# Recurrence of a four-mixer network: quarter-array products over four quarters, sums ahead of transposing, and a planner that keeps the time of each quarter

## The chip, the cores and the metric

The kernel runs on one core of a Trainium2 chip. The metric is the device time of one execution in microseconds (us); the times given are medians over executions.

The engines are called as the profile calls them: PE is TensorE (matrix products), PEld its loading of weights, DVE is VectorE, ACT is ScalarE, POOL is GpSimd, SP is SyncE, which issues most of the transfers. PSUM is the memory that PE writes into; it is used in banks of 128 x 512 float32, named `ps`. PE's array has 128 rows and 128 columns. A product with 64 rows and 64 columns of weights uses a quarter of the array, one with 128 rows and 64 columns half of it.

## The reference

One sequence of 512 tokens and width 1024 goes through four layers, each a mixer and a feed-forward part with the residual around both. The mixers are of four kinds: RWKV-7, attention in a window of 128 with sinks, a gated unit over chunks, and gated linear attention. The change is in the first of them, the RWKV-7 mixer, and in three helpers. Its core:

```python
def rmsnorm(x, g):
    y = x * lax.rsqrt(jnp.mean(jnp.square(x), -1, keepdims=True) + NORM_EPS)
    return y * g

def rwkv7_mix(x, ...):                    # 16 heads of 64
    ...                                   # r, w, k, v, a, g from products of x with weights
    def step(state, inp):                 # one token; state is 64 x 64 for each head
        r_t, d_t, k_t, v_t, kk_t, a_t = inp
        sa = jnp.einsum('bhvk,bhk->bhv', state, kk_t)
        state = (state * d_t[:, :, None, :]
                 - sa[..., None] * (kk_t * a_t)[:, :, None, :]
                 + v_t[..., None] * k_t[:, :, None, :])
        return state, jnp.einsum('bhvk,bhk->bhv', state, r_t)
    _, y = lax.scan(step, zeros, xs)
    ...                                   # mean and variance of y in each head
    y = ((y - mean) * lax.rsqrt(var + RW_GN_EPS)).reshape(B, S, D) * gn_g + gn_b
    bonus = (jnp.sum(r * k * r_k, -1, keepdims=True) * v).reshape(B, S, D)
    return ((y + bonus) * g) @ w_o
```

## The kernel before

**The program and its order.** The kernel is written as operations on engines that a class `Program` records (all of them through one helper, so that every operation has that helper's line in the profile: L365 before, L370 after). `Program.run` then sets the order by a simulated list schedule: each operation has a cost in ns and a turn, which is its number plus an offset from the table `TURNS` (ranges of numbers, each with an offset); of the operations that could start, the one with the earliest start, and among those the lowest turn, is taken next. The buffers come from pools with a fixed count, and the plan waits for a free one. Where PE would idle in the plan, `keep_warm` and `ahead_of_cold` put in products of the identity with itself (`ident`), whose results nobody uses; they are recorded at a line of their own (L647 before, L665 after) and are called fills here. Every engine then runs its list in this order on the chip; only semaphores make it wait there.

**Large products.** A product with float32 weights splits weights and tokens in two parts of fewer bits (`whi`, `wlo` from the loaded `wraw`), and multiplies them one by one. Nearly all time outside the recurrence goes to these.

**The start.** The mean of squares of each token is needed first. `token_squares` loads `x` by tokens in eight tiles (`slot<-x`), and squares and sums each on ACT or DVE; the vectors (`t<-vecs`) and the transposed `x` (`h<-x_t`) are loaded behind them. `rsqrt` computes 1/sqrt on DVE by three steps of Newton from an integer guess, `rstd` carries the factor of each token to a row over all partitions by products with the identity (`ident,rcol`), `h<-h,vec,ps` scales the tokens, and the first weight product (`slot,whi`) follows.

**The RWKV mixer.** After the products for k and r (`rf`, `kf`, 16 tiles named `rk`) the 16 heads go in four groups of four. For group `n`, `prepare(n)` makes decays and factors; `ahead(n)` makes the products of tokens with each other in chunks of 64 (`rwkv_products`, into `pr`/`pa`), the inverse of a triangular 64 x 64 block for each chunk and head (`rwkv_inverse`, by blocks of 16: two levels, each with 32 + 32 products of 64 x 64), and the direct part. `rwkv_chain(n)` then goes over the 512 tokens in eight steps (`b` of 0 to 3, `c` of 0 and 1), with the group's state `st` of 128 x 256:

- `ab`: products of `pa` with `v`, for two `b` at once; `xb`: products of the inverse (`iv`) with these;
- `x` gets the product of `qk` with the state; `vu` is copied from it by ACT;
- `pb`: the state by way of a product with the identity (`st,ident`, two of 128 x 128), to which four products `vu,et` of 64 x 64 are added; DVE multiplies by the decay `pend` into the next `st` (one operation of 128 x 256, or two of 64 x 128 for the first step of a group);
- four products `vu,pa` of 64 x 64 add the output `y` of the step.

`rwkv_out` normalises `y` in each head, transposes `y` and the bonus term (`yt`, `bt`, four transposes each for two `b`), and adds, scales and gates them on the transposed side. The chain of group `n` is recorded behind `prepare` and `ahead` of the next group, and the table mixes them. Then `rwkv_out_proj` multiplies the six first tiles with `rw_w_o` in the buffers of the recurrence (`et`), `stream` opens the buffers for large weights (`wraw` in the pool `wr`, eight of them, with `whi` and `wlo`), and `out_proj` does the last two tiles with these.

**In the first groups two of the four quarters work at a time:** the products of `ab` alternate between `(rows low, columns high)` and the opposite, those of `xb` between the other two; `vu,pa` of one step stay in one column half:

```python
halves = (lo, hi), (hi, lo)
...
mm(ab[ru, k * W:][:, hc(i, h)], pc(i, h, c, 1 - c, b + k)[rv], sb['v'][b + k][rv, hc(i, h)], ...)
mm(xb[:, c * W:(c + 1) * W][ru, hc(i, h)], inv(i, h)[ru], w1[ru, hc(i, h)], ...)
mm(x[rv, hc(i, h)], pc(i, h, c, c), vu[:, hc(i, h)], start=False, stop=True)
```

Of the kernel before, what the change touches and what calls it, by code (L numbers as in the profile page):

```python
# [9 lines left out]
F32 = mybir.dt.float32  # L10
# [7 lines left out]
P = 128  # L18
S = 512
# [301 lines left out]
class Program:  # L321

    WINDOW, SLACK, SEM, LOAD = 700, 200.0, 100.0, 95.0
    FREE, GAP, TAIL, TURN = 4, 450.0, 150.0, 92.0
    TICK, BUSY, DENSE, RICH = 10240 / 3, 3000.0, 3000.0, 4200.0

    def __init__(self, tc):  # L330
# [1924 lines left out]
```

## Time and profile before

| | |
|---|---|
| median of 3 executions | 2393.93 us (2393.26 to 2398.78) |
| the profiled execution | 2394.06 us, of which the span of the trace 2392.4 us |
| busy share of the span | PE 98%, PEld 82%, DVE 80%, ACT 60%, POOL 14% |
| granted TensorE clock | 9 tenths or more in all 40 slices of the page |
| transfers | 407.64 MB, mean 170 GB/s |

The profile is read in four stretches of the first layer's time, since only there something changes: the start until the first weight product (0 to 19.2 us), the dense products for r, k, v with the first group's preparation mixed into their end (to 222), the recurrence (222 to 380), the output projection (380 to 425). The other 1967 us hold the first feed-forward part and the other three layers. In a row of the timeline stand start, duration, engine, line, operation, `out<-in`, form, count, and in brackets how long the engine had been idle before it and on whom it waited.

### The profile page before, as it was taken

To read this page: it belongs to the slowest core of one execution; us is meant where nothing else is said; L and a number is where in the kernel's file an instruction comes from. 1 tells how busy PE (TensorE), PEld (TensorE's weight loads), DVE (VectorE), ACT (ScalarE), POOL (GpSimd) and SP (SyncE) were. 2 spreads that over 40 slices of the span, in tenths; PEclk is the share of its full clock that TensorE was granted. 3 is DMA by queue.
4 is the path that set the end of the run, shared out by engine and by line. 5 is a ranking of instruction groups with operands and counts; after the bars stand their busy time and mean duration, and the time that the engine had idled before them with its cause. 6 is when DMAs were issued, how large, how long until landed. Compare 5 with 4: busy or idle time off the path is not lost.

```text
span 2392.4 us, 36503 instructions
## 1 busy us (share of the span) xinstructions
PE 2354.2 (98%) x13756; PEld 1949.9 (82%) x13756; DVE 1913.3 (80%) x2974; ACT 1433.2 (60%) x2351; POOL 323.9 (14%) x388
## 2 busy tenths in 40 slices
PE   9999999999999999999999999999999999999998
PEld 7677789988888769888877888988888888888886
DVE  7687775886889789868688887877868978886868
ACT  4467784765556587655474444765556856765545
POOL 0000000211121011212121100212111111211211
PEclk9999999999999999999999999999999999999999
DMA  5220011889988268898888745888998877889885
GB/s 176 75 69 8 7 35 58 217 214 232 226 204 198 54 158 200 206 233 209 222 208 200 209 96 153 188 223 215 213 227 195 187 182 154 189 197 229 211 218 124
DMA packets 127681, 407.64 MB, mean 170 GB/s; under 512 B 14576, under 2 KB 19696, under 8 KB 127504
## 3 DMA queue, kind: packets, MB, share of 16 engines
q0 software_dynamic: 52992, 180.38, 42.2%
q1 hardware_dynamic: 74512, 224.93, 27.4%
q8 instruction: 108, 1.77, 0.3%
q14 instruction: 69, 0.57, 0.1%
HBM read 400.79 MB, written 2.10 MB: 168 GB/s over the span
## 4 chain that ended last, share of the span: by engine, by line
PE 87%; DVE 6%; ACT 4%; DMA 1%; issue 1%; SPq 0%; ACTq 0%; DVEq 0%
PE ps L365 87%; ACT et L365 2%; DVE slot L365 2%; ACT slot L365 1%; DVE wlo L365 1%; DVE et L365 1%; DMA wraw<-sg_w_u 1%; DVE h L365 0%; ACT whi L365 0%; DVE mx L365 0%; ACT vu L365 0%; DMA wraw<-ffn_w_b 0%; DMA slot<-x 0%; DVE ps L365 0%; DMA et<-rw_w_o 0%
## 5 line engine op out<-in xcount | busy, mean ns | idle before, releaser
L365 PE MATMUL ps<-whi,slot 128*128 128x512 f32 (+1 forms) x4944 | 1501.3, 384 | 0.5 <-DVE slot L365 0.3
L365 PEld LDWEIGHTS ps<-whi,slot 128*128 128x128 f32 x4944 | 918.7, 188 | 174.7 <-issue 7.8
L365 ACT CAST whi<-wraw 128x1024 fp32r<-128x1024 f32 (+2 forms) x683 | 677.8, 999 | 620.0 <-PE ps L365 518.9
L365 DVE TENSOR_TENSOR wlo<-wraw,whi 128x1024 fp32r<-128x1024 f32 (+2 forms) x683 | 782.8, 1157 | 233.1 <-ACT whi L365 223.8
L365 PE MATMUL ps<-wlo,slot 128*128 128x512 f32 (+1 forms) x2472 | 929.1, 383 | 1.4 <-DVE wlo L365 1.4
L365 PEld LDWEIGHTS ps<-wlo,slot 128*128 128x128 f32 x2472 | 463.8, 188 | 83.4 <-DVE wlo L365 5.0
L365 PE MATMUL ps<-slot,whi 128*128 128x512 f32 (+1 forms) x912 | 258.0, 369 | 5.2 <-ACT whi L365 2.3
L365 PEld LDWEIGHTS ps<-slot,whi 128*128 128x128 f32 x912 | 163.3, 190 | 39.7 <-ACT whi L365 4.8
L365 DVE TENSOR_TENSOR slot<-ps,slot 128x512 f32<-128x512 f32 (+1 forms) x238 | 150.3, 648 | 45.0 <-PE ps L365 41.2
L365 DVE TENSOR_TENSOR h<-h,ps 128x512 f32<-128x512 f32 x256 | 168.6, 684 | 18.6 <-PE ps L365 17.2
L365 POOL DMA_DIRECT2D wraw<-ffn_w_a x128 | 113.6, 893 | 480.6 <-DVE wlo L365 366.3
L365 DVE TENSOR_TENSOR slot<-left,slot 128x512 fp32r<-128x512 f32 (+1 forms) x252 | 159.9, 658 | 11.8 <-ACT slot L365 8.7
L365 PE MATMUL ps<-slot,wlo 128*128 128x512 f32 (+1 forms) x456 | 164.5, 367 | 0.8 <-DVE wlo L365 0.8
L365 ACT CAST slot<-left 128x512 fp32r<-128x512 f32 (+1 forms) x252 | 143.3, 599 | 33.7 <-DVE left L365 28.2
L365 ACT COPY slot<-ps 128x512 f32<-128x512 f32 (+2 forms) x157 | 82.8, 544 | 49.9 <-PE ps L365 39.0
L365 POOL DMA_DIRECT2D wraw<-ffn_w_b x64 | 55.9, 884 | 419.2 <-PE ps L365 224.1
L365 DVE TENSOR_TENSOR slot<-slot 128x512 f32<-128x512 f32 (+4 forms) x157 | 93.2, 617 | 11.0 <-DMA slot<-slot 6.5
L365 PEld LDWEIGHTS ps<-slot,wlo 128*128 128x128 f32 x456 | 85.7, 189 | 18.9 <-DVE wlo L365 3.0
L365 POOL DMA_DIRECT2D wraw<-ffn_o_a x64 | 55.3, 864 | 285.7 <-DVE wlo L365 176.9
L365 PE MATMUL ps<-ident,slot 128*128 128x128 f32 x524 | 87.0, 274 | 2.1 <-ACT slot L365 1.7
L365 DVE SCALAR_TENSOR_TENSOR slot<-slot,ncol 128x512 f32<-128x512 f32 (+1 forms) x96 | 66.8, 704 | 12.7 <-ACT slot L365 11.8
L365 PEld LDWEIGHTS ps<-ident,slot 128*128 128x128 f32 x524 | 62.9, 140 | 15.7 <-ACT slot L365 3.9
(282 smaller groups left out, 2085.3 us busy)
## 6 DMA issues: line engine op xcount, KB each, us to landing
wraw<-ffn_w_a SPq DMA_DIRECT2D x128, 512.0 KB, 5.9
wraw<-ffn_w_a POOLq DMA_DIRECT2D x128, 512.0 KB, 7.9
wraw<-ffn_o_a SPq DMA_DIRECT2D x64, 512.0 KB, 5.0
wraw<-ffn_o_a POOLq DMA_DIRECT2D x64, 512.0 KB, 7.0
wraw<-ffn_w_b SPq DMA_DIRECT2D x64, 384.0 KB, 5.4
wraw<-ffn_w_b POOLq DMA_DIRECT2D x64, 384.0 KB, 6.5
wraw<-ffn_o_b SPq DMA_DIRECT2D x16, 512.0 KB, 4.6
wraw<-ffn_o_b POOLq DMA_DIRECT2D x16, 512.0 KB, 6.8
```

The costliest lines, as they stand in the source:

```text
L365: op = self.add(eng.name, lambda: getattr(eng.target, what)(*map(real, args), **{k: real(a) for k, a in kw.items()}), *self.price(eng.name ...
```

## The change

1. **Planner.** `Program.run` keeps a time for each quarter of the array (`self.array`). A product of a quarter or half occupies its own quarters for its cost and lets PE go on after 13.5 ns (`STEP`); a change of form waits for all quarters and costs 92 ns from the full form or 140 ns into another (`shape`). Before, such a product cost half as much if the one ahead of it lay in the other half. The fills follow these times.
2. **TURNS** is a new table for the whole program, since the numbers of all operations move.
3. **Start.** `token_squares(xs)` takes the tiles of the transposed `x` (`h<-x_t`, now loaded first); the eight loads of `x` go. ACT squares the eight tiles, and PE sums over partitions by 32 products with one column of ones (`onec,slot`), into one PSUM column for each 128 tokens.
4. **`rsqrt`**, used in all layers: one step of higher order and one of Newton, eight DVE operations in place of ten.
5. **Pools.** `pa` and `mt` get pools of their own, `et` has 22 buffers instead of 30; `wr`, the raw weights' eight buffers, is opened before the last group's chain instead of in `stream`.
6. **`rwkv_inverse`.** The 64 x 64 products of both levels go round the four quarters (`turns`); the identity is added by a product `eye` at both levels (sixteen in place of eight), so that ACT copies the result of the first where DVE added.
7. **`rwkv_chain`.** The products of `ab` are recorded between those of `xb` (`other`). `st,ident` becomes four products of 128 rows and 64 columns for the two of 128 x 128. The `vu,pa` products of both steps of a `b` stand together, alternating in column halves. DVE's state update is always two operations of 64 x 128; the state has two buffers of each set.
8. **`rwkv_out`.** The factor `gn_g` is loaded as a row over all partitions (`gn`, one transfer for each group) and multiplied by token (eight new DVE operations of 128 x 512); the bonus is added before transposing, so its four transposes for two `b` go (32 in all).
9. **End.** In the last norm the first half of two tiles is scaled on ACT instead of DVE, its factor `g` being multiplied in earlier.

The diff, cut to what the text speaks of:

```diff
 TURNS = (
-    (0, 7, -1516), (7, 14, -753), (14, 38, -7759), (38, 44, -7766), ...
...
-EARLY = (("pa", 1), ("iv", 4), ("qk", 4))
-LATE = (("pr", 1), ("et", 30), ("vu", 4))
+EARLY = (("iv", 4), ("qk", 4))
+LATE = (("pr", 1), ("et", 22), ("vu", 4))
...
-                if op.form[:2] != self.form[:2]:
-                    cost += self.TURN
-                elif op.form[0] <= 64 and op.form[2] != self.form[2] or op.form[1] <= 64 and op.form[3] != self.form[3]:
-                    cost *= 0.5
-                self.form = op.form
+                part = [r * 2 + c for r in ((0, 1) if op.form[0] > 64 else (op.form[2] // 64,))
+                        for c in ((0, 1) if op.form[1] > 64 else (op.form[3] // 64,))]
+                s = max(s, self.shape(op.form), *[self.array[q] for q in part])
...
+                if len(part) < 4:
+                    now[e] = s + self.STEP
...
     def stream(self, slots):
-        self.weight_pools(8, 4, side="right")
+        self.wh = self.pool("wh", 4, side="right")
+        self.wl = self.pool("wl", 4, side="right")
...
     def rsqrt(...)
-        for _ in range(3):
-            nc.vector.tensor_mul(t, y, y)
-            nc.vector.scalar_tensor_tensor(t, x, -0.5, t, op0=ALU.mult, op1=ALU.mult)
-            nc.vector.scalar_tensor_tensor(y, t, 1.5, y, op0=ALU.add, op1=ALU.mult)
+        c = 3.0 / 8
+        nc.vector.tensor_mul(t, y, y)
+        nc.vector.tensor_mul(t, t, x)
+        nc.vector.scalar_tensor_tensor(t, t, -10.0 / 3, t, op0=ALU.add, op1=ALU.mult)
+        nc.vector.scalar_tensor_tensor(y, t, 5.0, y, op0=ALU.add, op1=ALU.mult)
+        ...                                   # one Newton step of three operations
...
-    def token_squares(self):
+    def token_squares(self, xs):
-        for j in range(2):
-            for b in range(NB):
-                x = self.slot()
-                nc.sync.dma_start(x, self.d['x'][b * P:(b + 1) * P, j * S:(j + 1) * S])
-                if b == NB - 1:
-                    nc.vector.bn_stats(st[:, j, :], x)
-                else:
-                    nc.scalar.activation(x, x, AF.Square, accum_out=ss[:, 2 * b + j:2 * b + j + 1])
+        for k, x in enumerate(xs):
+            sq = self.slot()
+            nc.scalar.activation(sq, x, AF.Square)
+            for b in range(NB):
+                nc.tensor.matmul(ps[:, b:b + 1], sq[:, b * P:(b + 1) * P], self.onec, start=k + b == 0, stop=k == KT - 1, ...)
...
+            if n == 3:
+                first.close()
+                self.wr = self.pool("wr", 8, side="right")
...
     def rwkv_inverse(...)
+        turns = (0, 0), (1, 1), (0, 1), (1, 0)
-            if lv:
-                for r in range(2):
-                    nc.tensor.matmul(ps[r], self.eye[0], ...)
+            for r in range(2):
+                nc.tensor.matmul(ps[r], self.eye[0], ...)
+            for f in range(2):
+                for jp in range(4):
+                    for r, e in turns:
+                        k, a = (e, f) if lv else (f, e)
+                        nc.tensor.matmul(ps[r][half[e], six(f * 4 + jp)], zk(k, r, 2 * jp + a), t0[f][half[r], six(2 * jp + e)], ...)
...
-                    u2 = self.part("mt")
-                    nc.vector.tensor_add(u2, u[k], ps[k])
+            for e in range(2):
+                nc.scalar.copy(u[e], ps[e])
...
     def rwkv_chain(...)
-                        for i in range(G):
-                            mm(pb[:, col(i)], self.ident, st[:, col(i)], start=i == 0, stop=False)
+                        for i, h in heads:
+                            mm(pb[h * 64:(h + 1) * 64, hc(i, h)], self.ident[:, h * 64:(h + 1) * 64], st[:, hc(i, h)], ...)
...
-                for i, h in heads:
-                    mm(x[rv, hc(i, h)], pc(i, h, c, c), vu[:, hc(i, h)], start=False, stop=True)
+                for i, h in heads:
+                    for c, (rv, ru) in enumerate(halves):
+                        mm(xb[:, c * W:(c + 1) * W][rv, hc(i, h)], pc(sb, b, i, h, c, c), vus[c][:, hc(i, h)], ...)
...
     def rwkv_out(...)
+            nc.vector.tensor_mul(two(y), two(y), sb['gn'].unsqueeze(1).to_broadcast([P, 2, W]))
+            nc.vector.tensor_add(y, y, bv)
-            yt, bt, gt = [self.bank() for _ in range(3)]
-            for t, x in ((yt, y), (bt, bv)):
+            yt, gt = [self.bank() for _ in range(2)]
...
-            nc.vector.tensor_add(o, o, bt)
```

In the lists below, `x4` is a run of four like instructions; a number such as in `st_2032` tells tiles of one name apart.

At the start of the program PE runs before the change:

```order
L647 MATMUL ps<-ident 128x128 x35
L365 MATMUL ps<-ident,t 128x128 x2
L647 MATMUL ps<-ident 128x128 x8
L365 MATMUL ps<-ident,rcol 128x128 x4
L647 MATMUL ps<-ident 128x128 x10
L365 MATMUL ps<-slot,whi 128x512 x4
```

After it (the first twelve rows, then the last four until the weight products):

```order
L665 MATMUL ps<-ident 128x128 x12
L370 MATMUL ps<-onec,slot 128x1 x4
L665 MATMUL ps<-ident 128x128
L370 MATMUL ps<-onec,slot 128x1
L665 MATMUL ps<-ident 128x128 x5
L370 MATMUL ps<-onec,slot 128x1 x5
L665 MATMUL ps<-ident 128x128 x2
L370 MATMUL ps<-ident,t 128x128
L370 MATMUL ps<-onec,slot 128x1
L370 MATMUL ps<-ident,t 128x128
L665 MATMUL ps<-ident 128x128 x3
L370 MATMUL ps<-onec,slot 128x1 x5
```

```order
L665 MATMUL ps<-ident 128x128 x8
L370 MATMUL ps<-ident,rcol 128x128 x4
L665 MATMUL ps<-ident 128x128 x8
L370 MATMUL ps<-slot,whi 128x512 x4
```

The 32 one-column products now stand ahead of `ident,rcol`, with fills between them: 22 of these products and 21 fills behind the first `ident,t`, and 8 more fills ahead of `ident,rcol`. The fills ahead of the first weight product go from 53 to 60.

In the recurrence, a stretch of the first group's chain on PE before:

```order
L365 MATMUL ps<-st_2000,h 128x128 x2
L365 MATMUL ps<-ident,h 128x128 x2
L365 MATMUL ps<-st_2000,ident 128x128 x2
L365 MATMUL ps<-vu,et 64x64 x4
L365 MATMUL ps<-vu,pa 64x64 x4
L365 MATMUL ps<-ident,h 128x128
```

And after:

```order
L370 MATMUL ps<-st_2032,h 128x128 x2
L370 MATMUL ps<-v_1524,pr 64x64
L370 MATMUL ps<-twa,wa 128x512
L370 MATMUL ps<-et,iv 64x64
L370 MATMUL ps<-st_2032,ident 64x64 x4
L370 MATMUL ps<-vu,et 64x64 x4
L370 MATMUL ps<-vu,pa 64x64 x8
L370 MATMUL ps<-v_1612,pa 64x64
L370 MATMUL ps<-et,iv 64x64
```

The state's product with the identity is in four parts of 64 columns, next to the four `vu,et` of the same form, and the `vu,pa` come eight at a time for both steps. Over the recurrence the changes of form on PE are 207 in place of 212.

At the end of `rwkv_out_proj` (`et,rk`) and the start of `out_proj` (`whi,rk`) PE runs before:

```order
L365 MATMUL ps<-et,rk 128x256 x157
L647 MATMUL ps<-ident 128x128 x20
L365 MATMUL ps<-whi,rk 128x512 x4
L365 MATMUL ps<-wlo,rk 128x512
```

And after:

```order
L370 MATMUL ps<-et,rk 128x256 x54
L665 MATMUL ps<-ident 128x128 x3
L370 MATMUL ps<-whi,rk 128x512 x5
L370 MATMUL ps<-wlo,rk 128x512
```

SP issues the transfers of these weights in this order before:

```order
L365 DMA et<-rw_w_o 128x2x256 x9
L365 DMA wraw<-rw_w_o 128x2x512 x2
L365 DMA wraw<-ffn_w_b 128x768 x16
```

And after:

```order
L370 DMA et<-rw_w_o 128x2x256 x7
L370 DMA wraw<-rw_w_o 128x2x512
L370 DMA et<-rw_w_o 128x2x256 x4
L370 DMA wraw<-rw_w_o 128x2x512
L370 DMA wraw<-ffn_w_b 128x768 x6
```

Both `wraw<-rw_w_o` move up between the loads into `et`, and 17 of the 20 fills go.

More of the change, by code (lines that the diff above doesn't have):

```diff
@@ L507, in run @@
             now[e] = end
+            if e == "PE":
+                for q in part:
+                    self.array[q] = end
+                if len(part) < 4:
+                    now[e] = s + self.STEP
             fin = end + op.lat
@@ L537, in run, with shape @@
                     bisect.insort(avail[o.eng], (o.turn, o.i, o))
-        self.time = max(now.values())
+        self.time = max(*now.values(), *self.array)
+    def shape(self, form):
+        t = 0.0
+        if form[:2] != self.form[:2]:
+            t = max(self.array) + (self.TURN if self.form[:2] == (P, P) else self.BACK)
+        self.form = form
+        return t
     def keep_warm(self, now, s, work):
@@ L544, in keep_warm @@
         free = pool.slots["ps"].free
-        if not first.done or not free or s - now < self.GAP:
+        if not first.done or not free or s - max(now, *self.array) < self.GAP:
             return now
-        t, n = max(now, min(free) + self.SEM), 0
+        t, n = max(now, min(free) + self.SEM, *self.array), 0
         while True:
-            c = 224.0 + (self.TURN if self.form[:2] != (P, P) else 0.0)
+            c = 224.0 + (self.BACK if self.form[:2] != (P, P) else 0.0)
             if work.get(int(t // self.TICK) - 1, 0.0) < self.BUSY:
@@ L561, in keep_warm @@
             self.fills += n
+            self.array = [now] * 4
         return now
@@ L1167, in rwkv @@
         nc, d = self.nc, self.d
-        ex, inner, early, wide, tall = [ExitStack() for _ in range(5)]
+        ex, inner, early, wide, tall, first = [ExitStack() for _ in range(6)]
         keepers = self.pool("rk", 16, ex)
@@ new lines, in other @@
+        def other(g, p):
+            ab = self.bank()
+            for k in range(2):
+                for i, h in heads:
+                    for c, (rv, ru) in enumerate(halves):
+                        mm(ab[ru, k * W:][:, hc(i, h)], pc(g, 2 * p + k, i, h, c, 1 - c)[rv], g['v'][2 * p + k][rv, hc(i, h)], start=k + i + h == 0, stop=True)
+                        yield
+            g['w2'] = self.part("wu")
+            nc.scalar.copy(g['w2'], ab)
+            yield
+        if n == 0:
+            for _ in other(sb, 0):
+                pass
```

211 lines of the change are left out of this document (104 added, 107 removed), and 261 rows, old and new, of the table TURNS.

## Prediction

> **What bounds the kernel now.** I read the busy shares first, then a table of stretches, since only the first 425 us hold changed work, and then for each stretch the waits, the chain and the timeline.
>
> ```profile
> PE 2354.2 (98%) x13756; PEld 1949.9 (82%) x13756; DVE 1913.3 (80%) x2974; ACT 1433.2 (60%) x2351; POOL 323.9 (14%) x388
> 165.00:222.00 57.00, 55.18 (x639) 39.70 (x639) 46.47 (x87) 33.20 (x55) 1.13 (x4) 1.00 0.07 20
> 222.00:380.00 158.00, 149.57 (x2396) 122.62 (x2393) 115.83 (x286) 124.56 (x275) 0.00 (x0) 1.00 0.12 38
> 380.00:425.00 45.00, 45.00 (x403) 43.83 (x402) 21.80 (x53) 10.69 (x24) 0.00 (x0) 1.00 0.12 42
> 425.00:2392.00 1967.00, 1944.26 (x9565) 1626.10 (x9563) 1607.75 (x2327) 1180.38 (x1876) 321.56 (x376) 1.00 0.81 193
> ```
>
> The stretches give PE, PEld, DVE, ACT and POOL busy, the granted clock, the DMA share and GB/s. PE is busy nearly throughout. In the recurrence (222 to 380) it idles 8.4 of 158 us, but ACT and DVE are busy 79% and 73% there too, and its chain says who carries the time:
>
> ```profile
> by line: PE ps L365 36.5%; ACT et L365 29.9%; DVE et L365 9.5%; ACT vu L365 4.8%; DMA et<-rw_w_o 4.0%; issue 2.5%; DVE h L365 1.9%; DVE qk L365 1.8%; ACT L365 1.6%; DVE pr L365 1.6%; DVE gvar L365 1.4%; DVE rs_t L365 1.4%; ACT rk L365 1.2%;
> PE ps L365 <- ACT et L365: 3.4, 6, 1.4
> PE ps L365 <- DVE et L365: 1.6, 4, 0.6
> ```
>
> PE holds 36.5% of that chain, copies out of PSUM a good part of the rest, while PE's own waits (us, times, longest) are few. So PE time taken away there shortens the stretch in part only.
>
> **PE work that goes in the recurrence.** A product of float32 is two records.
>
> ```profile
> 230.76 0.61 PE L365 MATMUL ps<-st,ident 128*128 128x128 f32 x4
> 231.30 0.45 PE L365 MATMUL ps<-vu,et 128*64 128x64 f32 x8
> 231.58 0.63 PE L365 MATMUL ps<-vu,pa 128*64 128x64 f32 x8
> 232.15 0.33 PE L365 MATMUL ps<-ident,h 128*128 128x128 f32 x1
> 245.21 0.66 PE L365 MATMUL ps<-ident,et 128*128 128x128 f32 x4
> 245.62 0.48 PE L365 MATMUL ps<-eye 128*128 128x512 f32 x1
> 245.94 0.60 PE L365 MATMUL ps<-ident,et 128*128 128x128 f32 x4
> 246.47 2.27 PE L365 MATMUL ps<-et 64*64 64x64 f32 x64
> 254.45 1.35 PE L365 MATMUL ps<-et 64*64 64x64 f32 x64
> ```
>
> Times are taken from start to start, since ends overlap.
> - Transposes: 4 records from 245.21 to 245.62, 0.103 each; 32 transposes less, 64 records: −6.6.
> - `vu,pa`: eight records in one column half take 231.58 to 232.15, 0.57; eight `vu,et` that alternate take 231.30 to 231.58, 0.28. 32 such groups now alternate: −0.29 x 32 = −9.3.
> - `st,ident`: four records from 230.76 to 231.30, 0.54, of which I leave 0.09 for the change of form that stays; eight records of the new form cost what `vu,et` does, 0.28: −0.17 x 24 = −4.1.
> - Inverse: the first level's 64 records take 2.27 in two quarters and 1.35 in four, as the second row shows: −0.92 x 4 = −3.7. Eight more `eye` products at 0.32 (245.62 to 245.94): +2.6.
> - `ab` products between those of `xb` could pair up too, but the new order puts them side by side only in places: 0.
>
> Sum −21.1; the first group's inverse runs ahead of the stretch, −0.3 of it, so −20.8 lie in 222 to 380, 0.13 for each us.
>
> **What of it comes through.** Where another engine is nearly full, it cannot.
>
> ```profile
> 222.00:242.00 20.00, 18.86 (x246) 15.80 (x246) 14.40 (x38) 18.91 (x42) 0.00 (x0) 1.00 0.00 1
> 242.00:262.00 20.00, 18.01 (x379) 13.65 (x371) 17.78 (x45) 11.58 (x26) 0.00 (x0) 1.00 0.01 3
> 262.00:282.00 20.00, 18.57 (x252) 14.77 (x250) 15.04 (x40) 19.64 (x43) 0.00 (x0) 1.00 0.05 16
> 302.00:322.00 20.00, 18.76 (x393) 15.87 (x390) 19.16 (x48) 15.87 (x40) 0.00 (x0) 1.00 0.03 9
> 362.00:380.00 18.00, 16.75 (x215) 14.88 (x207) 12.56 (x38) 12.65 (x31) 0.00 (x0) 1.00 0.42 136
> L365 ACT COPY et<-ps 128x512 f32<-128x512 f32 x44 | 24.9, 585 | 8.0 <-PE ps L365 7.7
> L365 DVE TENSOR_TENSOR st<-ps,pend x32: 277/424/426, 221.1 to 394.0; 128x256 f32<-128x256 f32 x24, 64x128 f32<-64x128 f32 x8
> ```
>
> The eight slices of 20 us each give up at most 2.6 us (2.4 for the last, of 18), and no more than the busier of ACT and DVE leaves free: 1.1 (ACT 18.91), 2.2 (DVE 17.78), 0.4 (ACT 19.64), 2.6, 0.8 (DVE 19.16), 2.6, 2.6, 2.4; the slices without a row have both other engines under 17. Sum −14.7. The ends are −7.6 (36.5% of 20.8) and −20.8. I take −14.7: it lets each slice go to what is really full in it, while the chain holds copies only because PE freed them late.
>
> ACT gets eight copies more, 8 x 0.585 = +4.7, in place of eight DVE additions; DVE's halves cost 24 x (2 x 0.277 − 0.424) = +3.1 more; its eight multiplications by `gn` stand against the eight additions that went, of the same size. That is hidden in the last three slices, where both have 4 to 10 us free; in the full ones it is the reason not to take more than −14.7. The four `gn` transfers stand on SP ahead of weights in stretches where the DMA share is 0.12: 0.
>
> The Trainium skill, in "TensorEngine Tiling (Array Packing)", section "PSUM Bottleneck", says that tiling speeds up TensorE and not the emptying of PSUM, so that the copy may become the bottleneck. The share of `ACT et` in the chain agrees; by that rule alone the gain would end nearer to the −7.6 above.
>
> **The wait ahead of the output projection.**
>
> ```profile
> 420.90 4.63 PE L647 MATMUL ps<-ident 128*128 128x128 f32 x40
> 422.09 1.04 ACT L365 CAST whi<-wraw 128x1024 fp32r<-128x1024 f32 x1 [16.36 <-DMA wraw<-rw_w_o]
> 425.28 0.94 PE L365 MATMUL ps<-whi,rk 128*128 128x512 f32 x3
> ```
>
> PE runs fills for 4.38 us (420.90 to 425.28) until the weight has landed and been split. The transfer could not start before `stream` opened its buffer. Now its buffer opens a group earlier, SP issues it before the last loads into `et`, and 3 fills stay (0.67): −3.7. If it lands late again, PE waits just as long: 0.
>
> **The start.** Here the change adds.
>
> ```profile
> 0.81 3.70 SPq L365 DMA_DIRECT2D slot<-x  x8
> 11.33 0.50 PE L365 MATMUL ps<-ident,t 128*128 128x128 f32 x2 [0.46 <-DMA t<-vecs]
> 12.88 0.17 DVE L365 TENSOR_SCALAR rcol<-ms 128x4 int32<-128x4 int32 x1
> 14.65 0.16 DVE L365 SCALAR_TENSOR_TENSOR rcol<-rs_t,rcol 128x4 f32<-128x4 f32 x1
> 14.87 0.65 PE L365 MATMUL ps<-ident,rcol 128*128 128x128 f32 x4 [1.25 <-DVE rcol L365]
> 15.36 2.40 PE L647 MATMUL ps<-ident 128*128 128x128 f32 x20
> 19.20 0.50 PE L365 MATMUL ps<-slot,whi 128*128 128x512 f32 x1 [1.45 <-ACT slot L365]
> 74.38 0.66 PE L365 MATMUL ps<-ident,t 8*128 8x8 f32 x8
> 74.97 0.50 PE L365 MATMUL ps<-slot,whi 128*128 128x512 f32 x1
> ```
>
> A fill is two records of 0.112 ((2.40 − 0.28)/19), 0.224. The vectors land behind eight tiles of the same size as before, so the first `ident,t` again waits until 11.33. Everything ahead of it (12 + 8 fills, 10 one-column products) is hidden by that wait. Behind it stand on PE, in this order and whether the data are there or not, 21 fills (4.7 us) and 22 one-column products, and DVE's sum waits for the last.
>
> No row shows such a product. Its weights are 128 x 128 as in a fill, its stream one column: at most like a fill, 0.224, as long as weights load beside the stream, and at least like two records of eight columns (74.38 to 74.97: 0.074 each), 0.148. I take the middle, 0.186: 22 x 0.186 = 4.1. So PE is done at 11.33 + 0.33 + 4.7 + 4.1 = 20.5, with 0.3 to drain; `ms` and eight operations of `rsqrt` at the spacing of 0.197 follow (ten, the first and last of which are quoted, start 1.77 apart, in nine steps), and `rcol` goes to PE at about 22.6, not 14.87: +7.7. From there to the first weight product it is 4.33 as before (8 fills in between take 1.8). PE is dense from there to 165, so the delay is not won back. Ends: +6.9 with 0.148; +29 if nothing overlaps (see the second rival).
>
> The Trainium skill, same page, section "Instruction Overhead", says that a product with one column lasts as long as one with 60, because of about 60 cycles of overhead. An estimate by that page is 0.105 us for four passes at 2.4 GHz; the start would be 1.8 us shorter and the sum 2380.9.
>
> **The rest.** In the tail two operations of `rsqrt` less, 0.197 each: −0.4. Between 425 and 2392 the work is the same in another order, PE idles 23 us of 1967 there, and I take 0, with ±4 as a bound (a fifth of that idle time).
>
> **Sum.** −14.7 − 0.3 − 3.7 + 7.7 − 0.4 = −11.4 on the profiled execution of 2394.06, which is 0.1 above the median: 2382.7. A measurement of this kernel tells about 0.3%, 7.2 us, from no change (2386.8 to 2401.1).
>
> **The rivals.**
> - *ACT and DVE carry the recurrence.* PE's share of the chain is all that counts, −7.6 in place of −14.7. For it: ACT at 18.91 and 19.64 of 20 in two slices, eight more copies. Against it: PE's waits for ACT and DVE are 6 us in all. Time 2389.8, within 0.3%.
> - *One-column products don't overlap with their weights* (the other side, slower). If weights load (PEld 0.19) and the product then drains (0.275) before the next, a record costs 0.465, a product 0.93 (both durations are the medians of a fill's records, below): 22 of them 20.5 instead of 4.1, and the ten ahead of the vectors, 9.3, overrun 11.33 by 5.3. The start costs +29, the time is 2404; slower by 0.3% from 0.83 for each product on. For it: no row of this form. Against it: the eight-column records, at 0.074, overlap.
>
> ```profile
> L647 PEld LDWEIGHTS ps<-ident x150: 186/192/333, 1.4 to 425.1; 128*128 128x128 f32 x150
> L647 PE MATMUL ps<-ident x150: 273/275/580, 1.4 to 425.2; 128*128 128x128 f32 x150
> ```
>
> - *PE alone carries the recurrence:* −20.8, the copies move up with it. For it: 149.57 of 158 busy. Time 2376.6.
> - *The clock is low behind the wait for the vectors.* PE idles some 2 us ahead of 11.33 in the new order, and early fills run slowly: 14 records in 3 to 5 us against 20 in 5 to 7.
>
> ```profile
> 3.00:5.00 2.00, 2.00 (x14) 2.00 (x13) 1.00 1.01 261
> 5.00:7.00 2.00, 2.00 (x20) 2.00 (x19) 1.00 0.91 298
> ```
>
> The granted clock reads 1.00 in both, so only the rate shows it. If PE ran at half rate again for the 8.8 us of fills and products, the start would cost +16.5: 2391.5, no measurable change. Against it: the wait is shorter than the first slow stretch. The Trainium skill, in "TensorE: Matmul & The Clock Gate", Part 1, says that the array halves its rate after an idle window of about 3.4 us; 2 us of waiting would then mostly not do it.
>
> **How the numbers follow.** Forecast 0.43; ACT and DVE carry it 0.20; PE carries it 0.20; low clock 0.08; no overlap 0.09 (with what the reordered rest may lose). Faster by over 0.3%: the forecast with most of its spread, 0.40, the PE rival 0.20, and a little of the second: 0.63. Within 0.3%: 0.18 + 0.07 and 0.03 of the forecast: 0.28. Slower: 0.09. The range reaches from the PE rival with −4 and the cheap start, and −4 of the rest (2376.6 − 0.8 − 4, rounded to 2370), to the first rival with the wait at the output projection kept (2389.8 + 3.7) and some of the rest, 2396. The forecast's own range, by the ends of the product's cost and ±4, is 2378 to 2387.
>
> **What would show it.** The first weight product at about 27 us; one-column products some 0.19 apart; the `vu,pa` groups of eight at 0.28 for each half; no long run of fills near 415; the recurrence some 15 us shorter with PE's share of its idle time unchanged or larger, waiting on ACT. Wrong would be: squares landing so late that the fills are free, a one-column product that costs much more, or new waits for buffers (`et` has eight less) inside the recurrence.

## The result, and the profile after

| | before | after |
|---|---|---|
| median | 2393.60 us (2391.91 to 2398.78) | 2365.02 us (2362.69 to 2366.38) |
| ratio | | 0.9876, interval 0.9859 to 0.9893 |
| span of the profiled execution | 2392.4 us | 2362.6 us |

The change made the kernel 28.6 us faster; the forecast was 11.4, and the time lies below the range. Two later executions at granted clocks of 0.28 and 0.85 are left out of the medians below. To see where the time went, I took events that are in both traces and read their starts: the first large weight product (`slot,whi`), the 500th large product behind it, the first product of the output projection (`whi,rk`), the last large product, and the end.

| from, to | before | after | difference | forecast |
|---|---|---|---|---|
| start, first large product | 19.2 | 26.0 | +6.8 | +7.7 |
| to the 500th (dense r, k, v products) | 146.6 | 141.1 | −5.5 | 0 |
| to the output projection (recurrence, its wait) | 259.5 | 236.3 | −23.2 | −18.7 |
| to the last large product (the rest) | 1956.9 | 1950.0 | −6.9 | 0 |
| to the end | 10.2 | 9.2 | −0.9 | −0.4 |
| sum | | | −29.7 | −11.4 |

The differences are taken before rounding. Six records of `twa,wa`, 2.0 us, moved from the recurrence to the dense stretch. With them put back, the dense stretch gained 7.5 and the recurrence 19.4 less 2.0 = 17.4, beside 3.8 from the wait at the output projection.

The table of stretches of the changed kernel, in the columns used before:

```profile
166.00:222.00 56.00, 54.67 (x716) 40.32 (x714) 47.39 (x107) 35.28 (x66) 1.09 (x4) 1.00 0.05 15
222.00:367.00 145.00, 133.79 (x2441) 106.72 (x2442) 117.64 (x284) 122.56 (x268) 0.00 (x0) 1.00 0.15 48
367.00:403.40 36.40, 36.40 (x318) 35.31 (x316) 23.57 (x60) 13.76 (x28) 1.92 (x2) 1.00 0.35 98
403.40:2362.00 1958.60, 1943.26 (x9562) 1623.65 (x9561) 1602.59 (x2300) 1179.96 (x1875) 320.57 (x374) 1.00 0.81 193
```

PE's busy time from 425 or 403 on is the same within 1 us, so nothing there became less work; its idle time fell from 22.7 us to 15.3. In the recurrence DVE and ACT do as much as before in less time. The timeline of PE at the start, in the recurrence and at the output projection:

```profile
10.52 0.27 PE L370 MATMUL ps<-ident,t 128*128 128x128 f32 x1
...
16.95 1.18 PE L370 MATMUL ps<-onec,slot 128*128 128x1 f32 x10
17.98 0.91 PE L665 MATMUL ps<-ident 128*128 128x128 f32 x6
...
20.21 2.03 PE L665 MATMUL ps<-ident 128*128 128x128 f32 x16
22.28 0.62 PE L370 MATMUL ps<-ident,rcol 128*128 128x128 f32 x4
22.74 1.95 PE L665 MATMUL ps<-ident 128*128 128x128 f32 x16
25.97 1.23 PE L370 MATMUL ps<-slot,whi 128*128 128x512 f32 x4 [1.28 <-ACT slot L370]
...
239.26 0.64 PE L370 MATMUL ps<-vu,pa 128*64 128x64 f32 x16
239.82 0.27 PE L370 MATMUL ps<-mt,pr 64*64 64x64 f32 x1
...
402.79 0.83 PE L665 MATMUL ps<-ident 128*128 128x128 f32 x6
403.37 1.41 PE L370 MATMUL ps<-whi,rk 128*128 128x512 f32 x5
```

Ten one-column records take 16.95 to 17.98, 0.103 each, 0.206 for a product. Eight output products (16 records) take 0.56, the 0.28 for eight records that the forecast had. Three fills are left at the output projection, for 0.58 us.

### The profile page after: what moved, and what is told of

Same layout as the page of the kernel before. It is cut to its first block, busy times and chain, and to the rows that moved or that the text cites. A ratio compares the mean times of both kernels' runs of the same rounds, so it can differ in the third digit from the quotient of the medians.

```text
span 2362.6 us, 36717 instructions
## 1 busy us (share of the span) xinstructions
PE 2331.4 (99%) x13868; PEld 1932.1 (82%) x13868; DVE 1908.6 (81%) x2948; ACT 1436.2 (61%) x2355; POOL 324.3 (14%) x386
## 4 chain that ended last, share of the span: by engine, by line
PE 88%; ACT 5%; DVE 5%; DMA 2%; issue 1%; POOL 0%; DVEq 0%; ACTq 0%; POOLq 0%
PE ps L370 87%; ACT et L370 2%; DVE slot L370 2%; ACT slot L370 1%; DVE wlo L370 1%; DMA wraw<-ffn_w_b 1%; DMA wraw<-ffn_w_a 1%; PE ps L665 1%; ACT vu L370 1%; DVE h L370 0%; DMA wraw<-sg_w_u 0%; ACT whi L370 0%; ACT left L370 0%; DVE left L370 0%; DVE mx L370 0%
## 5 line engine op out<-in xcount | busy, mean ns | idle before, releaser
L370 PEld LDWEIGHTS ps<-whi,slot 128*128 128x128 f32 x4944 | 918.1, 188 | 179.4 <-issue 10.6
L370 DVE TENSOR_TENSOR h<-h,ps 128x512 f32<-128x512 f32 x256 | 169.5, 684 | 18.7 <-PE ps L370 17.3
L370 PEld LDWEIGHTS ps<-ident,slot 128*128 128x128 f32 x524 | 62.8, 140 | 15.4 <-ACT slot L370 3.2
```

The costliest lines, as they stand in the source:

```text
L370: op = self.add(eng.name, lambda: getattr(eng.target, what)(*map(real, args), **{k: real(a) for k, a in kw.items()}), *self.price(eng.name ...
```

## The experiments

In most of them the order that the planner gave the changed kernel is written out as a list that `run` follows, so that an edit moves nothing else. Kernels with untouched recurrences reached the output projection up to 1.7 us apart, so smaller differences there mean nothing.

**The start: do the fills cost, and is the delay won back?** First, the 21 fills between one-column products were taken out:

```diff
-L665 MATMUL ps<-ident 128x128 x3        (seven of them, between the one-column products)
```

> The changed kernel in its own order, without the 21 fills that stand between the one-column products behind the first transpose of the vectors (21 x 0.224 = 4.7 us of PE). Theory A, PE is dense behind the start and its delay stays: the first weight product comes at 21.3 instead of 26.0 us, and the end moves by as much, 2365.0 - 4.7 = 2360.3. Theory B, the delay of the start is won back in the dense products, because without it they wait for data: the first weight product comes at 21.3 too, but the product that started at 96.0 still starts there, and the time stays at 2365. A mixed result would put the time between, and the landmark at 96 us says how much was won back.

2364.80 us, no gain; the first weight product came at 25.4, not 21.3. The timeline says why, and the windows behind it (the number behind PE's busy time is the granted clock), of this kernel and then of the changed one:

```profile
10.86 7.02 PE L508 MATMUL ps<-onec,slot 128*128 128x1 f32 x42
17.74 3.76 PE L694 MATMUL ps<-ident 128*128 128x128 f32 x16
```

```profile
11.00:13.00 2.00, 2.00 (x21) 1.00 0.88 348
13.00:17.70 4.70, 4.70 (x24) 0.50 0.62 193
17.70:21.30 3.60, 3.60 (x18) 0.50 0.52 148
```

```profile
11.60:20.20 8.60, 8.60 (x80) 1.00 0.67 213
20.20:22.20 2.00, 2.00 (x18) 1.00 0.09 29
```

Without fills the 42 records take 0.164 each on average instead of 0.103. Their starts are 0.112 us apart until 13.0; there the granted clock falls to 0.50, from then on they are 0.213 apart, and the 16 fill records behind take 3.76 instead of 2.03. Here one-column products back to back did not hold the clock, and the fills between them paid for themselves. Neither theory had this.

So the work itself had to go. The squared tiles were added on DVE, and 4 products remain:

```diff
-            for b in range(NB):
-                nc.tensor.matmul(ps[:, b:b + 1], sq[:, b * P:(b + 1) * P], self.onec, start=k + b == 0, ...)
+            if k:
+                nc.vector.tensor_add(sum_, sum_, sq)
+            else:
+                sum_ = sq
+        for b in range(NB):
+            nc.tensor.matmul(ps[:, b:b + 1], sum_[:, b * P:(b + 1) * P], self.onec, start=b == 0, ...)
```

> The changed kernel, with the eight squared tiles added up on DVE as they land (seven additions of 128 x 512), so that PE needs 4 one-column products instead of 32, and with fills set anew ahead of the first weight product; the order behind it is the same. The eighth square ends at about 10, the sum at 10.7, the vectors land at 10.5; the four products, ms, the reciprocal root and 4.3 us to the first weight product follow: it starts at about 18 instead of 26.0. Theory A, the delay of the start goes to the end: 2365.0 - 7.8 = 2357. Theory B, it is won back in the dense stretch: 2361 to 2365.

2356.84 us (2356.61 to 2357.81), ratio to before 0.9840 (0.9824 to 0.9856):

```profile
11.27 0.95 PE L508 MATMUL ps<-onec,slot 128*128 128x1 f32 x8
12.08 2.03 PE L694 MATMUL ps<-ident 128*128 128x128 f32 x16
14.06 0.65 PE L508 MATMUL ps<-ident,rcol 128*128 128x128 f32 x4
14.54 3.07 PE L694 MATMUL ps<-ident 128*128 128x128 f32 x26
```

The first weight product starts at 18.1, 7.9 earlier; the 500th is 7.1 earlier, the last 6.5. The start goes through to the end (theory A). No version here was faster beyond the runs' spread.

**The dense stretch.** What gained there? I first took the order of the kernel before for these operations:

> The changed kernel with the operations of the r, k and v products and the first group's preparation in the order of the kernel before, in which the half-array products stand in more and smaller groups between full ones. The start and the recurrence stay. Between the first weight product and the landmark at 166 us the change gained 5.5 us. Theory A, it is the order, which puts products of one form together: the time goes up by 5 to 6, 2370.5, and the rows of these products show it. Theory B, it is the delay of the start, which gives the transfers time, so that PE waits less: the time stays at 2365 within 1.

2387.88 us; the 500th product came 18.9 later, counted from the first, far more than the order cost before. In the timeline PE waits in places where the kernel before didn't, and the granted clock falls behind one of them:

```profile
157.13 1.07 PE L508 MATMUL ps<-slot,sel 128*64 128x512 f32 x2
161.40 1.16 PE L508 MATMUL ps<-h 64*128 64x128 f32 x16 [3.20 <-DVE h L508]
```

```profile
160.00:170.00 10.00, 8.60 (x34) 5.67 (x34) 3.95 (x6) 0.59 (x1) 0.00 (x0) 0.66 0.01 2
```

An old order on new buffers is neither kernel; the run says that the order counts, not how much it gained. The same holds for one line put back with the planner free:

```diff
-                    nc.tensor.matmul(ps[q], w[:, k * P:][:, q], blend(1 + 3 * c, k, self.slot()), ...)
+                    nc.tensor.matmul(ps[q], w[:, k * P:][:, q], blend(1 + 3 * c, k), ...)
```

> The changed kernel with one line back: the blended tokens of the half-array products with w1 and a1 go into the three buffers t again, not into slot; the planner orders it anew, and nothing behind the output projection moves. Theory A, these buffers made the dense stretch faster, since with three of them PE waits for blends and the half products stand in small groups between full ones: the product at 166 us comes 3 to 5 us later, the time is 2368 to 2370. Theory B, the dense stretch gained by the later start, which gave transfers and casts a lead: no change, 2365 to 2366.

2410.50 us, slower than before the change; the 500th product 48 us late. The table of offsets was made for other buffers. In the new plan 104 fill records stand ahead of that product, for 17.8 us, and PE waits 9.2 us, where the changed kernel has no fill and no wait; in places PE goes in step with the casts:

```profile
92.11 1.23 PE L370 MATMUL ps<-slot,whi 128*128 128x512 f32 x3 [0.23 <-ACT slot L370]
...
94.28 1.22 PE L370 MATMUL ps<-slot,whi 128*128 128x512 f32 x3 [0.24 <-ACT slot L370]
```

Narrower was a reordering within the runs of half-array products alone:

```diff
-    low, high, low, high, low, high, low, high      (column halves of a run of eight)
+    low, low, low, low, high, high, high, high
```

> The changed kernel in its own order, but within each of the three runs of half-array products with w1 and a1 (4, 3 and 8 of them) first all of one column half, then all of the other, so that they don't run in pairs: 7 pairs become 3. A pair takes 0.43 us, a product alone 0.43 too. Theory A, the dense stretch gained because half-array products stand side by side with both ready: 4 x 0.43 = 1.7 us later at the product that started at 96.0, and to the end, 2366.7. Theory B, they wait for their blends anyway: less than 0.5.

2366.60 us (2363.49 to 2371.50, so the time alone settles nothing); the product at 96.0 came 1.8 later, counted from the first weight product. Before the change, in the changed kernel and in this run, the timelines show:

```profile
80.22 2.99 PE L365 MATMUL ps<-t,wraw 128*64 128x512 f32 x8
83.14 0.50 PE L365 MATMUL ps<-slot,whi 128*128 128x512 f32 x1
```

```profile
73.58 1.94 PE L370 MATMUL ps<-slot,wraw 128*64 128x512 f32 x8
75.45 1.03 PE L370 MATMUL ps<-t,sel 128*8 128x512 f32 x4
...
79.24 3.65 PE L370 MATMUL ps<-slot,wraw 128*64 128x512 f32 x16
82.82 0.35 PE L370 MATMUL ps<-ident,t 8*128 8x8 f32 x3
```

```profile
79.89 5.42 PE L508 MATMUL ps<-slot,wraw 128*64 128x512 f32 x16
85.24 0.66 PE L508 MATMUL ps<-ident,t 8*128 8x8 f32 x8
```

The changed kernel's 16 records take 3.58 (79.24 to 82.82), since two halves run side by side; in the new order they take 5.35 (79.89 to 85.24), with eight records alone and four pairs left. Before, a run of eight took 2.92 (80.22 to 83.14), in the changed kernel 1.87 (73.58 to 75.45): part of it stood unpaired there. So the mechanism is shown, and its size in one run. My own reckoning of a pair was loose (a product alone takes 0.86, two records of 0.43, and the two shorter runs lost nothing), and the match with 1.7 is partly luck. Summed from each record's start to the next one's, the products with w1 and a1 cost 10.6 before and 8.3 after, `t,sel` 5.3 and 3.9, `slot,sel` 2.0 and 1.0: 4.7 of the 7.5. The other 2.8 lie in the full products `slot,whi` and `slot,wlo` themselves, 96.3 before and 93.5 after for 408 records each: a record next to one of another form mostly takes 0.32 us or more (as the one at 79.90 before, ahead of the first row above), the others take 0.23, and the half-array products now stand in fewer groups. All this is read from rows; only the 1.8 of the one run is tested.

**The recurrence: PE or ACT?** PE work put back, first the outputs by halves, then the inverse in two quarters, then both with the state's products as two of 128 x 128:

```diff
-                for i, h in heads:
-                    for c, (rv, ru) in enumerate(halves):      (output products alternate)
+                for c, (rv, ru) in enumerate(halves):
+                    for i, h in heads:
```

> The changed kernel in its own order, but in each group of eight output products of the chain first the four of one column half and then the four of the other, so that they no longer alternate. By the two traces this costs PE 8.2 us in the recurrence (18.4 us for these products before, 10.1 after). Theory A, PE carries the recurrence: the time goes up by about 8, to 2373. Theory B, ACT and DVE carry it and PE's work comes through by its share of the chain, 0.37: +3.0, 2368. The forecast's reading by slices, 0.7: +5.8, 2370.8.

> The changed kernel in its own order with the inverse's products in blocks of sixteen that use two quarters and then the other two, as in the run with all three put back; there they took 5.2 us more of PE than with the rotation. Theory A, each us of PE shows: 2370. Theory B, a good part is covered by waits for ACT: 2365 to 2367.5.

> The changed kernel in its own order with PE's work in the recurrence put back in three places: the output products by halves as in the run before, the state's product with the identity as two of 128 x 128, and the inverse's products in blocks of sixteen that use two quarters and then the other two. Putting back the outputs alone cost 4.2 us of PE and the recurrence became 4.3 longer. By the two traces the state's products cost 3.6 more before, the inverse's 10 more. Theory A, PE carries the recurrence and each us of it shows: 2365 + 4 + 4 + 10 = 2383. Theory B, copies carry it, PE comes through by its share of the chain: about 2371.5.

| run | time, us | PE put back (sum of its records) | output projection later |
|---|---|---|---|
| outputs by halves | 2367.27 | 4.1 | 4.3 |
| inverse in two quarters | 2367.51 | 4.2 | 3.1 |
| all three | 2372.42 | 13.0 | 8.1 |

0.6 us of each goes through over the three together, between the theories and near the forecast's 0.7. (The last time is close to theory B's 2371.5, but that counted on 18 us put back, not 13.) The 4.3 of the outputs hold up to 1.7 us of a low clock: the granted clock of that run is 0.83 from 280 to 290 us. Then ACT got more work and less:

```diff
                 nc.scalar.copy(tok, ps)
+                self.twice()                        (ACT does it again; in another run the copies into y)
```

> The changed kernel in its own order with ACT's copy of the tokens out of PSUM (tok, 128 x 512) done twice in each of the sixteen places of the chain: 16 x 0.585 = 9.4 us more of ACT in the recurrence, nothing more on PE. Theory A, PE carries the recurrence: the time stays within 1.5 us, 2365 to 2366.5. Theory B, ACT carries a third of it or more: 2368.3 up to 2374.

> The changed kernel in its own order with ACT's copies of the outputs y out of PSUM (64 x 256) done twice: 32 x 0.366 = 11.7 us more of ACT in the recurrence, at a place that the state doesn't wait for. Doubling the tok copies, which stand ahead of the state's vu copies on ACT, cost 13.5 us for 9.4. Theory A, ACT's sum of work carries the recurrence, wherever it stands: by the same slope +16.7, 2381.7. Theory B, only what stands ahead of the state's copies counts: less than +4, up to 2369.

> The changed kernel in its own order with less work on ACT in the recurrence: the bonus term's 64 operations of 64 columns (433 ns each, 27.7 us) become 16 plain copies of 256 columns (some 0.37 each, 5.9 us). The kernel leaves out the bonus factor and the centring. Nothing else moves, so PE idles no more than before and its clock is not in question. Theory A, ACT's sum of work carries the recurrence: 0.5 to 0.7 us for each us taken away, 2350 to 2355. Theory B, PE carries it and ACT hurts only where it is made later: 2362 to 2365.

| run | time, us | ACT's busy time | output projection |
|---|---|---|---|
| tok twice | 2378.16 | +9.3 | 13.6 later |
| y twice | 2377.03 | +11.8 | 14.0 later |
| bonus as plain copies | 2361.61 | −15.4 | 3.4 earlier |

The 64 operations taken out last 0.433 each but start some 0.33 apart, so that ACT's busy time falls by 15.4 and not by the 21.8 that was reckoned. The first two times lie above both theories for tok and between the two for y; taken alone, they would say that ACT carries it. The windows of the run with tok twice, and of the changed kernel, show something else beside it:

```profile
220.00:230.00 10.00, 10.00 (x94) 7.38 (x94) 6.01 (x23) 6.67 (x18) 0.00 (x0) 0.58 0.00 0
340.00:350.00 10.00, 8.38 (x150) 7.05 (x149) 6.76 (x15) 9.52 (x23) 0.00 (x0) 0.83 0.33 125
```

```profile
220.00:230.00 10.00, 9.04 (x137) 7.56 (x137) 8.83 (x29) 8.41 (x21) 0.00 (x0) 1.00 0.01 2
340.00:350.00 10.00, 9.71 (x281) 8.19 (x279) 6.28 (x17) 9.84 (x26) 0.00 (x0) 1.00 0.81 268
```

ACT late makes PE idle, and then PE's clock falls. What the granted clock lacks of 1.00 in the 10 us windows adds up to 10 us of PE time with tok twice and 5 with y twice. The rest is waiting: PE's idle time between the 500th product and the output projection is 12.5 us in the changed kernel, 16.5 with tok twice and 20.7 with y twice. So work added to ACT in this order is not free, even at a place that the state doesn't wait for. But without 15.4 us of ACT, where the clock stays, only 3.4 come back: the larger part of the recurrence is carried by PE. How much DVE carries is open: PE waits longest for DVE there (7.2 of 11.6 us between 166 and 403 in the changed kernel), and no run changed DVE's work alone. The windows of the run with less on ACT:

```profile
222.00:367.00 145.00, 136.89 (x2475) 109.70 (x2476) 119.72 (x288) 111.22 (x233) 0.00 (x0) 1.00 0.17 55
```

Moving the bonus to POOL, on top of the faster start, followed from theory A:

```diff
-                    nc.scalar.activation(bv[...], sb['v'][b][...], AF.Identity, scale=..., bias=...)      (64 of them)
+                nc.gpsimd.tensor_tensor(hw(o), hw(v4), wide(bonus), op=ALU.mult)                         (16 of them)
+                nc.gpsimd.tensor_tensor(hw(o), hw(o), wide(bm), op=ALU.add)
```

> The kernel with the squares added on DVE (2356.8), and the bonus term moved from ACT to POOL, which is idle in the recurrence: 32 operations of 128 x 256 instead of ACT's 64. Theory A, ACT carries the recurrence: 8 to 14 us less, 2343 to 2349. Theory B, PE carries it: 2354 to 2357. If POOL's work slows DVE, or the bonus comes too late for the addition, it is above 2357.

2358.50 us (2356.33 to 2359.07), no gain over 2356.84; theory A's 8 to 14 us are ruled out. That PE carries it is not shown by this run alone: ACT's busy time fell by 20.0 us between the 500th product and the output projection, but DVE's rose by 4.4 (its 128 x 16 operations on `rs_t` took 0.295 us beside POOL's work, 0.172 without), so part of a gain may have been lost there.

**The rest: order or shorter roots?** The order of before from the first feed-forward part on, then a narrower cut, then the roots with ten operations:

```diff
-    (operations 4940 to 16340 in the new order)
+    (the same in the order of the kernel before)
```

> The changed kernel with all operations from the first feed-forward part on in the order of the kernel before (PE's order exactly so); the two operations fewer of each reciprocal root stay. From 403 us on the change gained 6.9 us. Theory A, the new order is what gained there: the time goes back up by 6 to 7, 2371.5. Theory B, the shorter reciprocal roots and the shorter end gained it, some 0.4 us at each of the eleven places: the time stays at 2365 to 2367. What lies between says how the 6.9 are shared.

> As the run with the old order behind the recurrence, but cut so that only the operations from the end of the first feed-forward part to the start of the last mixer's end take the order of the kernel before; the last feed-forward part and the end keep the new one. In the earlier run the products fell behind by 7.2 us between 403 and 2295 us, and by 11 more in the last 60, where the two orders were joined badly. Theory A, the order gained the 6.9 us there: 2365 + 6 to 7 = 2371.5, without the 11. Theory B, the shorter reciprocal roots gained it: 2365 to 2366.

```diff
         nc.vector.tensor_mul(t, y, y)
+        self.twice()                                (both squares of a root)
```

> The changed kernel in its own order with the two squares of each reciprocal root done twice, so that a root has ten DVE operations again. Theory A, the two operations saved lie on the path at each norm: 0.4 us at some eleven places, 2369.4. Theory B, they are covered but at the start and the end: 2365 to 2366.

With the old order the time was 2385.05, with the narrower cut 2390.09: both joined badly in one place (11 us in the last 60, and 18 us near 2100), so the times say little. The traces say more. Of the weight products with 512 columns the 2000th came 0.3 earlier in the narrower cut than in the changed kernel, counted from the first, and the 5500th (at 1822.5 in the changed kernel) 7.6 later. Over that stretch, attention and gated unit for the most part, the change itself had gained 8.1 (from −18.3 to −26.4). So the old order gives back what the new one gained. The longer roots cost 1.1 us, 2366.14 (2365.80 to 2366.74), within the spread; no norm in the rest shows it. Theory A.

What the order gained are waits. From the output projection to the last large product, before and after:

```profile
425.28:2382.21 1956.93, 1943.59 (x9563) 1625.82 (x9561) 1602.21 (x2299) 1177.43 (x1872) 321.56 (x376) 1.00 0.81 193
403.37:2353.41 1950.04, 1942.90 (x9562) 1623.68 (x9561) 1598.19 (x2282) 1176.41 (x1869) 320.57 (x374) 1.00 0.81 193
```

PE's busy time stays, its idle time falls from 13.3 us to 7.1. More than half of that lies in one place, where the gated unit's weights (`sg_w_u`) come in: PE waits for a root, for a cast and for the low part of the weights, 4.0 us in all, and a low clock follows. The run with the old order behind the recurrence waits in the same place; the changed kernel starts these products without a wait. In this order: PE before the change, the window behind it with a granted clock of 0.62, the run with the old order, the changed kernel:

```profile
1258.76 0.62 PE L365 MATMUL ps<-ident,rcol 128*128 128x128 f32 x4 [1.23 <-DVE rcol L365]
...
1266.25 0.73 PE L365 MATMUL ps<-slot,whi 128*128 128x512 f32 x2 [2.28 <-ACT whi L365]
1267.51 0.80 PE L365 MATMUL ps<-slot,wlo 128*128 128x512 f32 x1 [0.53 <-DVE wlo L365]
```

```profile
1266.20:1270.70 4.50, 3.92 (x10) 2.81 (x11) 4.46 (x6) 2.74 (x5) 0.00 (x0) 0.62 0.52 178
```

```profile
1243.03 0.62 PE L509 MATMUL ps<-ident,rcol 128*128 128x128 f32 x4 [1.21 <-DVE rcol L509]
1250.39 0.73 PE L509 MATMUL ps<-slot,whi 128*128 128x512 f32 x2 [2.15 <-ACT whi L509]
1251.65 0.50 PE L509 MATMUL ps<-slot,wlo 128*128 128x512 f32 x1 [0.53 <-DVE wlo L509]
```

```profile
1234.92 0.61 PE L370 MATMUL ps<-slot,whi 128*128 128x512 f32 x2
1235.57 0.50 PE L370 MATMUL ps<-slot,wlo 128*128 128x512 f32 x1
```

## Why the prediction was wrong

- **The rest, "the same in another order ... I take 0, with ±4".** This step failed: −6.9. The bound was a fifth of PE's shown idle time, without a reason for a fifth. The new order took nearly half of what lies ahead of the last large product: idle time fell from 13.3 us to 7.1, busy time by 0.7. Most of what it took were waits that stand in the trace before the change, the longest ahead of 1266.25.
- **The dense stretch, costed at nothing.** Also failed: −7.5, moved work put back. I used "PE is dense from there" only to say that the delay isn't won back, which was right: the start's 7.9 us in the run with the added squares arrived at the end as 6.5. But I listed neither the blends' new buffers nor the half-array products' new neighbours among the edits, though before the change half-array products stood there unpaired. Here shown idle time bounds nothing: PE idled 0.2 of 146.6 us before, and records that run unpaired count as busy.
- **The recurrence, −15.0 of −21.1.** It came to −17.4. From the 500th product to the fills ahead of the output projection PE's busy time fell by 21.7, 2.0 of it moved, and its idle time rose by 2.3. The slices of 20 us took it that each slice's work stays in it; the planner moves work between slices, which may be why the bound was a little low (not tested). Among the terms: a transpose is one record, not two, so 32 of them are 3.3, not 6.6; the inverse gained 8.4 by its records from start to start (waits included), not 3.7, since all four runs of 64 records in each inverse became quicker, not one of them; the outputs −8.2 (forecast −9.3), the state −3.6 (−4.1), `eye` +2.2 (+2.6). The errors nearly cancel: that the sum was right is partly luck.
- **The output projection, −3.7:** −3.8. **The start, +7.7:** +6.8, with 0.206 for a one-column product where I took 0.186, and vectors landing 0.8 earlier. **The end, −0.4:** −0.9.
- **The rivals.** One-column products do overlap (0.206, not 0.93; the lower estimate of 0.105 is not borne out either). The rivals on ACT and on PE were about the share that comes through; the runs with a fixed order put 0.6 of PE's work on the path when it is put back, and 0.2 of ACT's when it is taken away. The low clock didn't come in the changed kernel, but it did as soon as the fills went. The Trainium skill, in "TensorE: Matmul & The Clock Gate", Part 1, has the half rate follow an idle window of some 3.4 us; the granted 0.50 agrees with the half rate, but not with the condition, since PE was shown as busy all through (11.0 to 17.7). The Trainium skill, in "TensorEngine Tiling (Array Packing)", "PSUM Bottleneck", says that the copy out of PSUM may become the bottleneck: 15.4 us of ACT less gave 3.4, so here ACT was not the bottleneck, though what went was the bonus term and not such a copy.

## What to carry to other kernels

Where a planner lays out a whole program anew, the gain is not the sum of the edits. List PE's waits in the trace before the change: the new order may remove any of them. Then look for products that use part of the array and stand unpaired, which count as busy, by the starts of records in each stretch against the best rate of the same form. When an experiment slows one engine, read the granted clock before you say who carries the time, and take work away as well as adding it. Sums of many small products are better added up on an idle engine first: here DVE added the eight tiles, 32 one-column products became 4, and the time fell by 8 us.

## What the runs showed of the hardware

- Float32 one-column products with 128 x 128 weights take 0.103 us a record in runs of ten with fills between them, at a granted clock of 1.00. Of 42 such records back to back, the granted clock fell to 0.50 some 2 us after the start, and the spacing went from 0.112 to 0.213.
- Two float32 products of 512 columns in opposite column halves start 0.007 us apart and take 0.43 for a record of each; alone each record takes its 0.43.
- A wait of 3.2 us on PE (158.2 to 161.4, the run with the old dense order) was followed by a mean granted clock of 0.66 from 160 to 170. Before the change, waits of 1.23, 2.28 and 0.53 us within 10 us were followed by a mean of 0.62 over 4.5 us.
